# Storing the float32 copy of h from ScalarE's queue instead of SyncE's

## The chip, the cores and the metric

One Trainium2 chip, one core of it. The metric is the device time of one execution in microseconds; before and after are each given as a median of several executions. Beside the timed executions there is one profiled execution of the kernel before, and everything that is read from a trace comes from that one.

## What is computed

One decoder layer over 1024 tokens of 1024 channels, in float32. The part around the change is its beginning:

```python
ada = jax.nn.silu(c) @ w_ada + b_ada
shift, scale, gate = jnp.split(ada, 3, axis=-1)
h = _rmsnorm(x, norm_w) * (1.0 + scale[:, None, :]) + shift[:, None, :]
proj = jnp.einsum("bsd,de->bse", h, w_in)
z_ssm, xbc, dt_raw, q, k, v, z_att, f_logit, g_logit = jnp.split(proj, offsets, axis=-1)
y_ssm = _ssd_branch(z_ssm, xbc, dt_raw, conv_w, conv_b, dt_bias, a_log, d_skip, ssm_norm_w)
y_att = _fox_branch(q, k, v, z_att, f_logit, b_f)
g_ssm, g_att = jnp.split(jax.nn.sigmoid(g_logit + b_gate), N_BRANCHES, axis=-1)
merged = g_ssm * jnp.einsum("bse,ed->bsd", y_ssm, w_proj_ssm) + g_att * jnp.einsum("bse,ed->bsd", y_att, w_proj_att)
x = x + gate[:, None, :] * jnp.einsum("bsd,de->bse", merged, w_out)
return _rmsnorm(x, final_norm_w)
```

So h needs the row norms of x (over channels) and the two vectors scale and shift, which are products of silu(c) with a 1024 x 2048 matrix. All that follows is products of h with w_in, a state-space branch, an attention branch and the closing products.

## The kernel before, in words

Every product is done in split precision: a float32 matrix is cut into a high part (`hi`, a cast on ScalarE, L98) and a low part (`lo`, a subtraction on VectorE, L99), and TensorE forms hi·hi, hi·lo and lo·hi. Such a triple is L111, L112, L113 in `c_half`.

The opening stage builds h, transposed: eight blocks `k` of 128 channels, each in two halves `hf` of 512 tokens. Its parts are:

- Loads, all from SyncE's queue: eight pieces of x (`xt`, L209, 512 KB each), eight pieces of w_ada (`wa`, L213, 1 MB each, in five buffers), and the weights of the first three slabs (`wr`, L217).
- Row norms (L257 to L261): ScalarE squares and sums a piece of x (`sq`), VectorE and GpSimd form the factor `rs`, ScalarE scales the piece in place (L261). Eight pieces.
- `ada_cols(k)`: VectorE multiplies and adds eight pieces of one `wa` tile (L285 once, L287 seven times, into `acc`), two one-column products on TensorE sum it over partitions (`cp`, L289), VectorE forms the columns `av` and `sv` (L292, L294).
- `h_half(k, hf)`: four transposes on TensorE into the single buffer `tp` (L300), the activation that scales and shifts and writes `xa` in float32 (L303, ScalarE, four buffers), the store of `xa` to `h_scr` in DRAM (L304), the cast to the high part `hh` (L305, ScalarE) and the subtraction to the low part `hl` (L306, VectorE). That is 16 halves, so 16 stores of 256 KB.
- While h grows, TensorE multiplies each finished half with the first three slabs (L111 to L113 into the banks `mm` and `um`).

The float32 copy `h_scr` is read back once, at the start of the next stage, by `t_forms` (L441), which forms differences of blocks of h.

The program hands its instructions to a scheduler (`schedule_with_timeline_sim=True`), which writes one list per engine; each engine runs its list in order. DMAs are issued from such a list too, here all from SyncE's. The build also deals the DMAs out, one after the other, over eight completion counters, `DMAHW0` to `DMAHW7`. A DMA waits for its counter before it is issued: for the DMA that had the counter eight places before it.

Of the kernel before, what the change touches and what calls it, by code (L numbers as in the profile page):

```python
# [65 lines left out]
def build(ctx, tc, t):  # L66
    nc = tc.nc
    V, A, G, PE, SP = nc.vector, nc.scalar, nc.gpsimd, nc.tensor, nc.sync
# [7 lines left out]
    def f32(ap):  # L76
        return ap.bitcast(F32)
# [88 lines left out]
    h_scr = [dram.tile([P, S], F32, name=f"h_scr{k}") for k in range(NK)]  # L166
# [27 lines left out]
    def w_in(n, i, p):  # L194
        if (n, i, p) in ws_scr:
            return unit(ws_scr[n, i, p], 512)
        return unit(t["w_" + n][p + 4 * (i == 4), i % 2 == 0 and 1 or 0], 512)


    with tc.tile_pool(name="st", bufs=1, side="right") as st, \  # L200
# [95 lines left out]
        def h_half(k, hf):  # L296
            fs = slice(hf * 512, (hf + 1) * 512)
            tp = stp.tile([P, 512], F32, tag="tp", bufs=1, name="tp")
            for i in range(4):
                PE.transpose(out=tp[:, i * P:(i + 1) * P], in_=xts[4 * hf + i][:, k * P:(k + 1) * P],  # L300
                             identity=ident)
            xa = st.tile([P, 512], F32, tag="xa", bufs=4, name="xa")
            A.activation(out=xa, in_=tp, func=AF.Identity, scale=av[:, k:k + 1], bias=sv[:, k:k + 1])  # L303
            SP.dma_start(out=h_scr[k][:, fs], in_=xa)  # L304
            A.copy(out=hh[k][:, fs], in_=xa)  # L305
            V.tensor_tensor(out=hl[k][:, fs], in0=xa, in1=f32(hh[k][:, fs]), op=ALU.subtract)  # L306

        for k in range(2):
            ada_cols(k)
            h_half(k, 0)  # L310
        for k in range(2):
            h_half(k, 1)
        for k in range(2, 8):
            ada_cols(k)
            for hf in range(2):
                h_half(k, hf)
# [784 lines left out]
    with tc.tile_pool(name="finp", bufs=1, space=PSUM) as fpp_:  # L1101
# [66 lines left out]
        for i in ORDER:  # L1168
# [17 lines left out]
            else:  # L1186
                fs = [w_in("o", i, k) for k in range(4)]
# [65 lines left out]
```

## Time and profile before

| what | value |
|---|---|
| time, median of 3 executions | 1218.62 us (1217.94 to 1220.36) |
| the profiled execution | 1224.31 us, of it 1222.6 us span |
| busy: TensorE, VectorE, ScalarE, GpSimd | 1165.0, 955.9, 635.5, 88.4 us |
| mean granted TensorE clock | 0.988 |
| stores of `xa` (L304) | 16 of 256 KB, issued from 26.2 to 69.2 us |
| opening stage | from 0 to about 71 us of the span |

The span is what lies between the first and the last instruction of the profiled execution; 1.7 us of that execution's own time lie around it. That execution took 5.7 us more than the median of the timed ones. In rows of the timeline the first number is the start, the second the length, both in us; then engine, line and operation, output and input, and in brackets the idle time of the engine before it with what ended it. "SPq" and "ACTq" are the instruction lists of SyncE and ScalarE as far as they issue DMAs or wait. An `x7` at the end says that seven such instructions are drawn together.

### The profile page before, as it was taken

Reading aid. Unit: us, or ns where it says so; the run is one execution under the profiler, and the core shown is the slowest. Engines: PE = TensorE matmul, PEld = TensorE weight load, DVE = VectorE, ACT = ScalarE, POOL = GpSimd, SP = SyncE. Lnnn points to the kernel's source line nnn. Section 1 sums busy time; section 2 is a strip of 40 time slices with the busy share of each in tenths; the row PEclk is TensorE's granted clock in tenths of the full one; section 3 lists DMA queues with packets and bytes.
Section 4 is the critical chain, followed back from the end, with each engine's and each line's share of the span. In section 5 each row is a group of like instructions: output and inputs, shape, how many; then the busy total and the mean of one; then the engine's idle time right before and its main releaser. Section 6 shows DMA issues by size and latency. Waiting matters only on the chain.

```text
span 1222.6 us, 18382 instructions
## 1 busy us (share of the span) xinstructions
PE 1165.0 (95%) x6206; PEld 981.2 (80%) x6206; DVE 955.9 (78%) x1946; ACT 635.5 (52%) x1260; POOL 88.4 (7%) x152
## 2 busy tenths in 40 slices
PE   3999999999999999999999989999988999999997
PEld 2788888788877877998887778888877887788876
DVE  5856699788987784589999986664677977989967
ACT  7554443454443334776676633454456554454465
POOL 1000000000000000000000012222322220000001
PEclk9999999999999999999999989999998999999999
DMA  9665643655485676546545668422246526875334
GB/s 370 263 243 166 218 138 100 207 204 176 156 290 171 218 239 201 186 152 222 186 154 178 207 216 286 144 94 81 87 165 203 175 88 228 283 241 181 109 95 147
DMA packets 109018, 228.26 MB, mean 187 GB/s; under 512 B 12362, under 2 KB 20220, under 8 KB 107900
## 3 DMA queue, kind: packets, MB, share of 16 engines
q1 hardware_dynamic: 108924, 227.09, 55.2%
q8 instruction: 49, 0.80, 0.3%
q14 instruction: 45, 0.37, 0.1%
HBM read 159.14 MB, written 67.90 MB: 186 GB/s over the span
## 4 chain that ended last, share of the span: by engine, by line
PE 62%; DVE 16%; DMA 13%; ACT 4%; issue 4%; SPq 1%; POOL 0%; POOLq 0%; DVEq 0%; ACTq 0%
PE pp L497 4%; PE pv L1067 4%; PE pp L499 4%; PE pp L500 4%; PE lg L1036 3%; PE mm L497 3%; PE mm L499 3%; PE mm L500 3%; PE mm L112 3%; PE mm L113 3%; PE mm L111 3%; PE tp L1057 2%; DMA ab<-a_scr 2%; DMA wr<-w_c 2%; PE mm L919 2%
## 5 line engine op out<-in xcount | busy, mean ns | idle before, releaser
L98 ACT CAST wh<-wr 128x512 fp32r<-128x512 f32 (+1 forms) x214 | 131.0, 620 | 176.2 <-DMA wr<-w_c 32.4
L99 DVE TENSOR_TENSOR wl<-wr,wh 128x512 fp32r<-128x512 f32 (+1 forms) x214 | 146.9, 693 | 44.0 <-ACT wh L98 43.3
L112 PE MATMUL mm<-hl,wh 128*128 128x512 f32 x288 | 116.7, 405 | 0.4 <-DVE hl L306 0.4
L111 PE MATMUL mm<-hh,wh 128*128 128x512 f32 x288 | 116.2, 408 | 0.0
L113 PE MATMUL mm<-hh,wl 128*128 128x512 f32 x288 | 115.5, 402 | 0.0
L136 PE MATMUL mm<-wh,hh 128*128 128x256 f32 (+1 forms) x256 | 73.7, 289 | 1.9 <-DVE tmp L348 1.9
L137 PE MATMUL mm<-wl,hh 128*128 128x256 f32 (+1 forms) x256 | 74.4, 291 | 0.0
L138 PE MATMUL mm<-wh,hl 128*128 128x256 f32 (+1 forms) x256 | 73.7, 289 | 0.0
L1042 ACT ACTIVATE pr<-pr,sm 128x1024 f32<-128x1024 f32 (+3 forms) x64 | 49.9, 780 | 42.4 <-DVE sm L1041 35.1
L1060 ACT CAST pth<-tp 128x512 fp32r<-128x512 f32 (+1 forms) x80 | 42.4, 543 | 47.7 <-PE tp L1057 39.5
L1037 DVE CUSTOM_DVE_ANT_0 pr<-lg,fb 128x512 f32<-128x512 f32 (+1 forms) x96 | 51.4, 552 | 17.0 <-PE lg L1036 12.4
L112 PEld LDWEIGHTS mm<-hl,wh 128*128 128x128 f32 x288 | 55.2, 192 | 11.0 <-DVE hl L306 1.0
L113 PEld LDWEIGHTS mm<-hh,wl 128*128 128x128 f32 x288 | 55.0, 191 | 10.4
L111 PEld LDWEIGHTS mm<-hh,wh 128*128 128x128 f32 x288 | 54.7, 193 | 10.2 <-ACT hh L305 0.3
L690 ACT ACTIVATE ab<-ab,acs 128x128 f32<-128x128 f32 x128 | 41.2, 391 | 40.7 <-DMA ab<-a_scr 40.5
L1045 POOL TENSOR_SCALAR pr<-pr,sm 128x1024 f32<-128x1024 f32 (+3 forms) x64 | 51.8, 811 | 87.5 <-DVE sm L1044 70.2
L1061 DVE TENSOR_TENSOR ptl<-tp,pth 128x512 fp32r<-128x512 f32 (+1 forms) x80 | 50.0, 632 | 10.3 <-ACT pth L1060 10.2
L98 ACT CAST sh<-sr 128x512 fp32r<-128x512 f32 x57 | 34.0, 619 | 43.8 <-DVE sr L479 32.4
L796 POOL TENSOR_TENSOR fl<-fl,mhalf 128x8 f32<-128x8 f32 x1 | 1.6, 1647 | 698.2 <-DVE fl L794 698.2
L136 PEld LDWEIGHTS mm<-wh,hh 128*128 128x128 f32 x256 | 48.8, 191 | 2.4 <-DVE tmp L348 2.2
L1067 PE MATMUL pv<-pth,vh 128*128 128x256 f32 (+1 forms) x160 | 45.8, 287 | 4.5 <-DVE zg L1070 3.8
L138 PEld LDWEIGHTS mm<-wh,hl 128*128 128x128 f32 x256 | 49.1, 192 | 0.0
(407 smaller groups left out, 3509.8 us busy)
## 6 DMA issues: line engine op xcount, KB each, us to landing
wr<-w_c SPq DMA_DIRECT2D x116, 256.0 KB, 3.9
wa<-w_ada SPq DMA_DIRECT2D x8, 1024.0 KB, 11.4
g_scr<-gt SPq DMA_DIRECT2D x16, 512.0 KB, 4.2
ab<-a_scr SPq DMA_DIRECT2D x32, 256.0 KB, 3.9
gt<-g_scr SPq DMA_DIRECT2D x32, 256.0 KB, 3.7
wr<-w_ps SPq DMA_DIRECT2D x28, 256.0 KB, 2.6
wr<-w_pa SPq DMA_DIRECT2D x28, 256.0 KB, 2.8
wr<-so SPq DMA_DIRECT2D x28, 256.0 KB, 2.7
```

The lines of the kernel that those rows point to most:

```text
L98: A.copy(out=hi[:, :n], in_=raw[:, :n])
L99: eng.tensor_tensor(out=lo[:, :n], in0=raw[:, :n], in1=f32(hi[:, :n]), op=ALU.subtract)
L111: PE.matmul(ps, lhsT=hi[:, cs], rhs=xh[k][:, hs], start=(k == 0), stop=False)
L112: PE.matmul(ps, lhsT=hi[:, cs], rhs=xl[k][:, hs], start=False, stop=False)
L113: PE.matmul(ps, lhsT=lo[:, cs], rhs=xh[k][:, hs], start=False, stop=(k == 7))
L136: PE.matmul(o, lhsT=xh[k][:, ts], rhs=hi[:, cs], start=(k == 0), stop=False)
L137: PE.matmul(o, lhsT=xh[k][:, ts], rhs=lo[:, cs], start=False, stop=False)
L138: PE.matmul(o, lhsT=xl[k][:, ts], rhs=hi[:, cs], start=False, stop=(k == 7))
L497: PE.matmul(ps, lhsT=f[0][:, w], rhs=xh[:, hs], start=(first and k == 0), stop=False, skip_group_check=True)
L499: PE.matmul(ps, lhsT=f[0][:, w], rhs=xl[:, hs], start=False, stop=False, skip_group_check=True)
L500: PE.matmul(ps, lhsT=f[1][:, w], rhs=xh[:, hs], start=False, stop=(k == 3), skip_group_check=True)
L1067: PE.matmul(pv[:, o0:256], lhsT=x[kb // 4][:, kb % 4, vs], rhs=y[:, d:d + m], start=(kb == 0 and i == 0), stop=(kb == 2 * qq + 1 and i == 2))
```

## The change

The store at L304 is issued from ScalarE's list instead of SyncE's:

```diff
             xa = st.tile([P, 512], F32, tag="xa", bufs=4, name="xa")
             A.activation(out=xa, in_=tp, func=AF.Identity, scale=av[:, k:k + 1], bias=sv[:, k:k + 1])
-            SP.dma_start(out=h_scr[k][:, fs], in_=xa)
+            A.dma_start(out=h_scr[k][:, fs], in_=xa)
             A.copy(out=hh[k][:, fs], in_=xa)
             V.tensor_tensor(out=hl[k][:, fs], in0=xa, in1=f32(hh[k][:, fs]), op=ALU.subtract)
```

The scheduler then writes other lists, and three places matter.

First, ScalarE, right behind the first activation of the opening stage (`xa_421`, block 0, first half). Names are tiles with their buffer numbers; the bracket names the counters that the row waits for, `DMAHW7` being the one that the load `wa_292` used before. In the kernel before:

```order
L305 CAST hh0_240<-xa_421 128x512 [waits Activation_49]
L257 ACTIVATE sq_348,ss_323<-xt_282 128x1024 [waits DMAHW2_49]
L257 ACTIVATE sq_354,ss_323<-xt_284 128x1024 [waits DMAHW3_49]
L261 ACTIVATE xt_282<-xt_282,rs_350 128x1024 [waits Activation_49,Pool_49]
L257 ACTIVATE sq_360,ss_323<-xt_286 128x1024 [waits DMAHW4_49]
L261 ACTIVATE xt_284<-xt_284,rs_356 128x1024 [waits Activation_49,Pool_49]
L257 ACTIVATE sq_366,ss_323<-xt_288 128x1024 [waits DMAHW5_49]
L98 CAST e2_388<-wr_280 128x512 [waits DMAHW1_49]
L303 ACTIVATE xa_445<-tp_440,sv_373,av_372 128x512 [waits DVE_49,PE_49]
L261 ACTIVATE xt_286<-xt_286,rs_362 128x1024 [waits Activation_49,Pool_49]
L261 ACTIVATE xt_288<-xt_288,rs_368 128x1024 [waits Activation_49,Pool_49]
L305 CAST hh1_241<-xa_445 128x512 [waits Activation_49]
```

The same place in the changed kernel, again right behind the activation that writes `xa_421`:

```order
L304 DMA h_scr0_179<-xa_421 128x512 [waits DMAHW7_49,Activation_49]
L257 ACTIVATE sq_348,ss_323<-xt_282 128x1024 [waits DMAHW2_49]
L305 CAST hh0_240<-xa_421 128x512
L257 ACTIVATE sq_354,ss_323<-xt_284 128x1024 [waits DMAHW3_49]
L261 ACTIVATE xt_282<-xt_282,rs_350 128x1024 [waits Activation_49,Pool_49]
L257 ACTIVATE sq_360,ss_323<-xt_286 128x1024 [waits DMAHW4_49]
L303 ACTIVATE xa_445<-tp_440,sv_373,av_372 128x512 [waits DVE_49,PE_49]
L261 ACTIVATE xt_284<-xt_284,rs_356 128x1024 [waits Activation_49,Pool_49]
L257 ACTIVATE sq_366,ss_323<-xt_288 128x1024 [waits DMAHW5_49]
L98 CAST e2_388<-wr_280 128x512 [waits DMAHW1_49]
L261 ACTIVATE xt_286<-xt_286,rs_362 128x1024 [waits Activation_49,Pool_49]
L304 DMA h_scr1_180<-xa_445 128x512 [waits DMAHW1_49,Activation_49]
```

The first store now stands directly behind its activation, ahead of the norms of the last four pieces of x and of the first cast to `hh`; behind the last row shown come the cast of `hh1_241` and then the scaling of `xt_288`.

Second, SyncE, around the same stores; `wa_304` and `wa_306` are the loads of the seventh and eighth pieces of w_ada, `wr_844` and those after it the next stage's first weights. A minus marks rows of the kernel before that are gone from this list:

```order
 L217 DMA wr_298<-w_c 128x512
-L304 DMA h_scr0_179<-xa_421 128x512
 L213 DMA wa_304<-w_ada 128x2048
-L304 DMA h_scr1_180<-xa_445 128x512
-L304 DMA h_scr0_179<-xa_455 128x512
-L304 DMA h_scr1_180<-xa_465 128x512
 L213 DMA wa_306<-w_ada 128x2048
 L85 DMA wr_844<-w_v0 128x560
 L85 DMA wr_850<-w_v0 128x560
 L85 DMA wr_856<-w_v0 128x560
-L304 DMA h_scr2_181<-xa_489 128x512
 L85 DMA wr_862<-w_v0 128x560
```

The loads keep their order, and no store stands between them any more; the other stores are gone from the rows after these in the same way.

Third, VectorE between the second low part of block 2 and the first of block 3 (`hl_250` and `hl_251`). Before:

```order
L306 TENSOR_TENSOR hl_250<-xa,hh_242 128x512
L287 SCALAR_TENSOR_TENSOR acc<-wa,cols,acc 128x256 x7
L306 TENSOR_TENSOR hl_250<-xa,hh_242 128x512
L287 SCALAR_TENSOR_TENSOR acc<-wa,cols,acc 128x256 x2
L306 TENSOR_TENSOR hl_251<-xa,hh_243 128x512
```

In the changed kernel, from the second `hl_250` on:

```order
L306 TENSOR_TENSOR hl_250<-xa,hh_242 128x512
L287 SCALAR_TENSOR_TENSOR acc<-wa,cols,acc 128x256
L292 SCALAR_TENSOR_TENSOR av<-cp,cols 128x1
L294 TENSOR_TENSOR sv<-cp,cols 128x1
L285 TENSOR_SCALAR acc<-wa,cols 128x256
L287 SCALAR_TENSOR_TENSOR acc<-wa,cols,acc 128x256 x2
L99 TENSOR_TENSOR wl<-wr,wh 128x560
L287 SCALAR_TENSOR_TENSOR acc<-wa,cols,acc 128x256
L292 SCALAR_TENSOR_TENSOR av<-cp,cols 128x1
L294 TENSOR_TENSOR sv<-cp,cols 128x1
L285 TENSOR_SCALAR acc<-wa,cols 128x256
L287 SCALAR_TENSOR_TENSOR acc<-wa,cols,acc 128x256 x4
```

Sums for later blocks have moved ahead of `hl_251`, which follows the last row. Elsewhere the lists differ at two more places, one pair of loads in the attention of the third head (SyncE's rows L812 and L1022 are exchanged) and the order of some casts and products in the closing product; GpSimd's list is the same.

## Prediction

> **What bounds the kernel now.** I read the page first, then the busy time by stretches of the opening stage, then the timelines of ScalarE, SyncE, VectorE and TensorE there. The page:
>
> ```profile
> span 1222.6 us, 18382 instructions
> PE 1165.0 (95%) x6206; PEld 981.2 (80%) x6206; DVE 955.9 (78%) x1946; ACT 635.5 (52%) x1260; POOL 88.4 (7%) x152
> ...
> PE 62%; DVE 16%; DMA 13%; ACT 4%; issue 4%; SPq 1%; POOL 0%; POOLq 0%; DVEq 0%; ACTq 0%
> ```
>
> TensorE is busy for 95% of the span, so whatever delays its dense work moves the end by as much. The change touches only the opening stage, so I look there, cut where the argument needs it (columns: length, then busy us and count for PE, PEld, DVE, ACT, POOL, then clock and DMA):
>
> ```profile
> 18.25:26.20 7.95, 4.71 (x15) 4.01 (x16) 3.68 (x13) 7.92 (x13) 2.44 (x4) 1.00 1.03 421
> 29.07:71.00 41.93, 41.15 (x205) 33.56 (x206) 31.83 (x77) 24.16 (x38) 0.00 (x0) 1.00 0.61 231
> 80.00:90.00 10.00, 8.06 (x51) 7.83 (x50) 9.27 (x19) 4.20 (x9) 0.00 (x0) 0.83 0.95 371
> ```
>
> From 18.25 to 26.20 us ScalarE is the full engine (7.92 of 7.95 us) and TensorE has gaps (4.71). From 29.07 to 71 us TensorE is full: 41.15 of 41.93 us, so at most 0.78 us can be made good there. Early on ScalarE sets the pace, later TensorE.
>
> **The change part by part.** *The store's wait.* What the store waited for on SyncE:
>
> ```profile
> 12.19 2.86 SPq L213 DMA_DIRECT2D wa<-w_ada  x2
> ...
> 26.20 0.33 SPq L304 DMA_DIRECT2D h_scr<-xa  x1
> 26.86 0.33 SPq L213 DMA_DIRECT2D wa<-w_ada  x1
> ...
> 33.48 0.33 SPq L213 DMA_DIRECT2D wa<-w_ada  x1
> ```
>
> ```profile
> SPq L304 <- DMA wa<-w_ada: 2.1, 1, 2.1
> ```
>
> ```profile
> wa<-w_ada SPq DMA_DIRECT2D x1, 1024.0 KB, 11.4
> ```
>
> The first of these is SyncE's timeline, the second its waits between 24.1 and 26.3 us, the third the landing time of the second load of the pair at 12.19. That load (`wa_292`) is issued at 12.19 + 2.86 - 0.33 = 14.7 us and lands 11.4 us later, at 26.1. The store goes out at 26.20, and its wait is put down to a `wa` load. That agrees with the lists: the store waits for `DMAHW7`, which `wa_292` had. The data of the store has nothing to do with that load. On SyncE this cost nothing; in the changed kernel the same wait stands in ScalarE's list. Nothing that SyncE issues ahead of it is moved, so `wa_292` lands at 26.1 again.
>
> What stands behind it on ScalarE, from the timeline:
>
> ```profile
> 17.45 0.78 ACT L303 ACTIVATE xa<-tp,sv,av 128x512 f32<-128x512 f32 x1
> 18.25 0.62 ACT L305 CAST hh<-xa 128x512 fp32r<-128x512 f32 x1
> 18.78 1.05 ACT L257 ACTIVATE sq<-xt 128x1024 f32<-128x1024 f32 x1
> ...
> 19.83 1.04 ACT L257 ACTIVATE sq<-xt 128x1024 f32<-128x1024 f32 x1
> ...
> 25.16 0.60 ACT L98 CAST e<-wr 128x512 fp32r<-128x512 f32 x1
> 25.66 0.77 ACT L303 ACTIVATE xa<-tp,sv,av 128x512 f32<-128x512 f32 x1
> 26.34 2.17 ACT L261 ACTIVATE xt<-xt,rs 128x1024 f32<-128x1024 f32 x2
> 28.42 0.60 ACT L305 CAST hh<-xa 128x512 fp32r<-128x512 f32 x1
> ```
>
> Does such a wait hold the engine? A wait of ScalarE's list ahead of an activation:
>
> ```profile
> L303 ACTq EVENT_SEMAPHORE  x14: 17/17/1991, 15.4 to 66.7; - x14
> ```
>
> ```profile
> 37.29 0.78 ACT L303 ACTIVATE xa<-tp,sv,av 128x512 f32<-128x512 f32 x1 [1.97 <-DVE sv L294]
> ```
>
> The longest wait of the list, 1.991 us, is the same 1.97 us for which the engine stood idle. So ScalarE stands from 18.25 to 26.20, 7.95 us, in the very stretch in which it was full. The rows give the starts from one instruction to the next: activation 0.80, cast to hh 0.53, square 1.05, scaling 2.08 / 2 = 1.04, cast `e` 0.50. For the issue I take SyncE's 0.33; the trace has no store issued by ScalarE, and its bounds are 0 and 0.38 (the row of all 16, below). Up to the cast of `hh1`, the changed list has: two issues 0.66, four squares 4.20, one cast 0.53, three scalings 3.12, one activation 0.80, one cast `e` 0.50, in sum 9.81. That cast starts at 26.20 + 9.81 = 36.0 instead of 28.42: **7.6 us later** (the wait and two issues, less one scaling that has moved behind it). Who waits for it: VectorE (the norms' factors and `hl`), GpSimd (`rs`) and TensorE, none of which has other work to fill the time, since TensorE's dense stretch begins with these products at 29.07.
>
> *TensorE's order.* Its timeline while slow and while fast:
>
> ```profile
> 33.08 0.63 PE L112 MATMUL mm<-hl,e 128*128 128x512 f32 x1
> 33.51 0.52 PE L113 MATMUL mm<-hh,e 128*128 128x512 f32 x1
> 33.86 0.62 PE L111 MATMUL um<-hh,wh 128*128 128x512 f32 x2
> ...
> 35.46 0.40 PE L112 MATMUL um<-hl,wh 128*128 128x512 f32 x1
> 35.69 0.39 PE L113 MATMUL um<-hh,wl 128*128 128x512 f32 x1
> ...
> 41.02 0.50 PE L112 MATMUL mm<-hl,wh 128*128 128x512 f32 x1 [0.44 <-DVE hl L306]
> ...
> 47.41 0.48 PE L112 MATMUL mm<-hl,wh 128*128 128x512 f32 x1
> ```
>
> A product takes 0.43 us from start to start up to about 33.9 us and 0.23 after. Before, the first `um` product came 33.86 - 28.42 = 5.4 us after the start of that cast. In the changed list the last transpose of the next half stands behind all nine products of `hh1`: cast 0.62, nine products 3.9, transpose 0.4, activation 0.80, issue 0.33, cast 0.62, in sum 6.7. That is **1.2 us more**; bounds 0 (the products already fast: 9 x 0.20 = 1.8 less) and 3.6 (twelve products more at the slow spacing, 12 x 0.20 = 2.4).
>
> The Trainium skill (TensorE: Matmul & The Clock Gate, Part 1) has the array at half clock until it has been busy for about 3.4 us. The trace agrees in kind (0.43 against 0.23), though the granted clock reads 1.00 throughout. By that rule the new gaps while TensorE waits for ScalarE keep it slow for longer, which is the upper of the two bounds; I keep the middle.
>
> *VectorE's order.* Rows around the low parts of blocks 2 and 3:
>
> ```profile
> 40.29 0.68 DVE L306 TENSOR_TENSOR hl<-xa,hh 128x512 fp32r<-128x512 f32 x1
> 40.89 2.85 DVE L287 SCALAR_TENSOR_TENSOR acc<-wa,cols,acc 128x256 f32<-128x256 f32 x7
> 43.66 0.68 DVE L306 TENSOR_TENSOR hl<-xa,hh 128x512 fp32r<-128x512 f32 x1
> ...
> 45.06 0.68 DVE L306 TENSOR_TENSOR hl<-xa,hh 128x512 fp32r<-128x512 f32 x1
> ...
> 47.18 0.21 DVE L292 SCALAR_TENSOR_TENSOR av<-cp,cols 128x1 f32<-128x1 f32 x1
> ...
> 47.63 0.74 DVE L99 TENSOR_TENSOR wl<-wr,wh 128x560 fp32r<-128x560 f32 x1
> 48.28 2.04 DVE L287 SCALAR_TENSOR_TENSOR acc<-wa,cols,acc 128x256 f32<-128x256 f32 x4
> ```
>
> From the first `hl` of block 2 to that of block 3 passed 45.06 - 40.29 = 4.8 us. The changed list puts four more sums there (4 x 2.77 / 7 = 1.6 us), two groups of columns and a first product (0.45 each, 47.18 to 47.63) and one `wl` (0.65): 3.1 us more, 7.9 in all. TensorE needed 6.4 us for its own work between the two (its products with them start at 41.02 and 47.41) and gets 0.3 of columns more, so it waits about **1.2 us**; bounds 0 and 3.1.
>
> *The later stores.* Fourteen issues stand ahead of their casts, up to 0.38 us each:
>
> ```profile
> L304 SPq DMA_DIRECT2D h_scr<-xa x16: 319/320/383, 26.2 to 69.2; - x16
> ```
>
> ```profile
> ACT xa L303 <- PE tp L300: 12.7, 10, 2.9
> ```
>
> ScalarE waited 12.7 us for transposes in that stage, which covers fourteen issues (5.3 us at most): I cost them at nothing. Without that cover, each would push its cast and cost up to 5.3 us. One of them waits for the counter of `wa_306`, which by my count is issued at 40 us, with the store due at 48. The load at 33.48 landed in 9.1 us:
>
> ```profile
> wa<-w_ada SPq DMA_DIRECT2D x1, 1024.0 KB, 9.1
> ```
>
> So 40 + 9.1 - 48, about 1 us, is at stake there. *SyncE's list* loses its waits, and the last `wa` and the first weights of the next stage may leave earlier; nobody waits for them on TensorE before 71 us. The exchanges further on I cost at nothing, within some 2 us either way (the size of the single wait in the row of the first rival): which of their waits end last is not to be read from lists.
>
> The sum: 7.6 + 1.2 + 1.2 = 10.0 us. The profiled execution took 1222.6 us of span and 1.7 around it; with 10.0 more it would take 1234.3. It is 5.7 above the median of 1218.62, so the forecast goes on the median: **1228.6 us**.
>
> **The rivals.** *Faster: the loads freed from the stores.* The place is SyncE: `wa` at 26.86 and 33.48 stood behind stores and left late. If ScalarE were not held, for example were the load of `DMAHW7` to land by 18 us, the next stage would find its data ready and this wait would go:
>
> ```profile
> PE mm L136 <- DVE tmp L348: 1.9, 1, 1.9
> ```
>
> With the 0.78 us above that is at most 2.7 us: 1215.9. It decides only if the counter is free within 2.7 us of 18.25. Against it stands the landing at 26.1.
>
> *No change: the store costs its issue time only.* Nothing on TensorE's path then moves, and the time stays at 1218.6. For it speaks that SyncE issued such stores in 0.33 us; against it the 1.97 us row. The Trainium skill (DMA: Bandwidth & Descriptors, "Issuing engines are not separate DMA queues") says that issuing from several engines only saves the sequencer's time for starting transfers; by it nothing is gained but SyncE's time. No run here shows a second issuing engine.
>
> *Half: the hold is absorbed.* TensorE's gaps before 29 us take up more than I count, and the waits of the first rival go as well: 7.6 - 2.7 = 4.9, 1223.5.
>
> *More: waits multiply.* The upper bounds of both orders, 7.6 + 3.6 + 3.1 = 14.3: 1232.9.
>
> **How the numbers follow.** Forecast (6 to 13 us slower) 0.75; more than that 0.06; half 0.10; no change 0.05; faster 0.04. A measurement of this kernel tells about 0.2% (2.4 us) from no change. So slower 0.91, same 0.05, faster 0.04. The range goes from the half case, 1223.5, to the upper bounds, 1233.0, and leaves out about 0.15.
>
> **What would show it.** Right: ScalarE idle from about 18.2 to 26.2 us behind the first `xa`, ended by a `wa` load; the cast of `hh1` near 36 us; TensorE's full stretch starting about 8 us later and ending near 81 instead of 71; the rest unchanged in length. Wrong: ScalarE squaring the fifth piece of x at 19 us, which is one of the first two rivals; or the hold there and the end less than 3 us later, which would mean slack that I did not find.

## The result and the profile after

The changed kernel took 1230.53 us (median of 6 runs, 1225.4 to 1233.06), the kernel before 1220.28 beside it (6 runs, 1217.94 to 1221.01): the ratio on record is 1.0078 with a 95% interval of 1.0054 to 1.0102 (the two medians alone give 1.0084). The forecast was 1228.6, which is 10.0 above the first median of before. The profiled execution took 1229.29 us, of it 1227.5 span, at a mean granted clock of 0.993 (before: 1224.31, 1222.6, 0.988). So the timed runs are 10.25 us apart and the profiled ones 5.0; why, is a question of its own below. Two later executions of the kernel before took 1734.67 and 1908.23 us at a granted clock of 0.619 and 0.563; they are left out of all that follows.

First the page of the changed kernel:

```profile
span 1227.5 us, 18378 instructions
PE 1161.4 (95%) x6206; PEld 977.3 (80%) x6206; DVE 953.6 (78%) x1946; ACT 633.8 (52%) x1260; POOL 87.1 (7%) x152
```

TensorE's busy time is 3.6 us less and the span 4.9 more: what was added is waiting. Where, is in the busy time of the three stretches that were shown of before:

```profile
18.25:26.20 7.95, 2.13 (x8) 1.64 (x8) 2.11 (x5) 0.37 (x1) 0.00 (x0) 1.00 1.03 418
29.07:71.00 41.93, 37.56 (x168) 29.18 (x168) 32.52 (x86) 25.51 (x40) 1.86 (x3) 0.96 0.58 208
80.00:90.00 10.00, 10.00 (x69) 9.32 (x69) 4.78 (x8) 7.15 (x13) 0.00 (x0) 1.00 0.76 228
```

From 18.25 to 26.20 ScalarE is busy for 0.37 us instead of 7.92, while the DMA engines move what they moved before (418 GB/s against 421). TensorE's full stretch has lost 3.6 busy us and 37 of its 205 products. ScalarE's timeline shows what stands there (`ACTq` is the issue of a store; in brackets the idle time and what ended it):

```profile
17.85 0.78 ACT L303 ACTIVATE xa<-tp,sv,av 128x512 f32<-128x512 f32 x1
26.63 0.34 ACTq L304 DMA_DIRECT2D h_scr<-xa  x1
27.02 1.06 ACT L257 ACTIVATE sq<-xt 128x1024 f32<-128x1024 f32 x1 [8.39 <-DMA wa<-w_ada]
...
32.37 1.14 ACT L261 ACTIVATE xt<-xt,rs 128x1024 f32<-128x1024 f32 x1
32.75 0.33 ACTq L304 DMA_DIRECT2D h_scr<-xa  x1
...
36.01 0.60 ACT L305 CAST hh<-xa 128x512 fp32r<-128x512 f32 x1
...
71.07 0.78 ACT L303 ACTIVATE xa<-tp,sv,av 128x512 f32<-128x512 f32 x1 [0.73 <-DVE hl L306]
71.88 0.33 ACTq L304 DMA_DIRECT2D h_scr<-xa  x1
72.25 0.62 ACT L305 CAST hh<-xa 128x512 fp32r<-128x512 f32 x1 [0.40 <-ACT xa L303]
```

The square behind the first store starts after 8.39 us of idle time, which a load of w_ada ends; in the kernel before, the same square started at 18.78 without a wait. The second store at 32.75 is issued while ScalarE is still scaling a piece of x (32.37 to 33.51): its list runs ahead of the arithmetic, and the next square, at 33.41, shows no idle time before it. A store straight behind its activation, as at 71.88, leaves 0.40 us between activation and cast; without a store it was 0.02 (17.45 + 0.78 to 18.25 in before). ScalarE's waits from 16 to 85 us, in all, times, longest:

```profile
ACT xa L303 <- PE tp L300: 12.1, 7, 2.7
ACT sq L257 <- DMA wa<-w_ada: 8.4, 1, 8.4
ACT hh L305 <- ACT xa L303: 4.8, 12, 0.4
```

One wait on a load, and twelve of 0.4 us behind stores. TensorE's products at the places that the prediction named, and VectorE's first low parts of blocks 2 and 3:

```profile
28.73 1.22 PE L111 MATMUL mm<-hh,wh 128*128 128x512 f32 x2 [7.19 <-ACT hh L305]
...
42.87 0.74 PE L111 MATMUL um<-hh,wh 128*128 128x512 f32 x2 [0.35 <-ACT hh L305]
...
50.68 0.39 PE L112 MATMUL mm<-hl,wh 128*128 128x512 f32 x1
...
58.36 0.50 PE L112 MATMUL mm<-hl,wh 128*128 128x512 f32 x1 [0.80 <-DVE hl L306]
```

```profile
49.00 0.69 DVE L306 TENSOR_TENSOR hl<-xa,hh 128x512 fp32r<-128x512 f32 x1
...
57.62 0.68 DVE L306 TENSOR_TENSOR hl<-xa,hh 128x512 fp32r<-128x512 f32 x1
```

The end of the opening stage is marked by SyncE's first load of `pe`, which waits for the last stores. It was at 71.36 us before; in the changed kernel:

```profile
81.55 1.75 SPq L441 DMA_DIRECT2D pe<-h_scr  x4
```

That is 10.2 us later.

### The profile page after: what moved, and what is told of

It reads as the page before. It is cut to its first block, busy times and chain, and to the rows that moved or that the text cites. A ratio compares the mean times of both kernels' runs of the same rounds, so it can differ in the third digit from the quotient of the medians.

```text
span 1227.5 us, 18378 instructions
## 1 busy us (share of the span) xinstructions
PE 1161.4 (95%) x6206; PEld 977.3 (80%) x6206; DVE 953.6 (78%) x1946; ACT 633.8 (52%) x1260; POOL 87.1 (7%) x152
## 4 chain that ended last, share of the span: by engine, by line
PE 62%; DVE 14%; DMA 13%; ACT 5%; issue 4%; SPq 1%; ACTq 0%; POOL 0%; POOLq 0%; DVEq 0%
PE pv L1067 4%; PE pp L497 4%; PE pp L499 4%; PE pp L500 4%; PE lg L1036 3%; PE mm L497 3%; PE mm L499 3%; PE mm L500 3%; PE mm L112 3%; PE mm L111 3%; PE mm L113 3%; DMA ab<-a_scr 2%; PE tp L1057 2%; DMA wa<-w_ada 2%; PE mm L919 2%
## 5 line engine op out<-in xcount | busy, mean ns | idle before, releaser
L137 PEld LDWEIGHTS mm<-wl,hh 128*128 128x128 f32 x256 | 48.2, 188 | 0.2
```

The source lines that it names most:

```text
L137: PE.matmul(o, lhsT=xh[k][:, ts], rhs=lo[:, cs], start=False, stop=False)
```

## The experiments

The theory: ScalarE is held at the first store, by a completion counter that a w_ada load has, and the rest follows. The main rival: every store on ScalarE costs (issue time, and the lists re-ordered around it). A second question came from the trace: how much of the opening's loss stays to the end. In all runs two marks show the opening stage: the start of the second block's cast (`hh1`), and the first `pe` load. "Timed" is the median less that of the kernel before beside it.

| kernel | cast of `hh1` | first `pe` load | timed, us | ratio, 95% |
|---|---|---|---|---|
| before; once more | 28.42; 28.72 | 71.36; 70.87 | 0; +1.8 | 0.9995 to 1.0028 |
| changed; once more | 36.01; 35.79 | 81.55; 81.31 | +10.3; +7.9 | 1.0054 to 1.0102; 1.0042 to 1.0086 |
| only the first store on ScalarE; once more | 35.64; 35.73 | 79.83; 80.09 | +5.4; +4.5 | 1.0029 to 1.0063; 1.0021 to 1.0054 |
| all but the first | 29.88 | 73.07 | -0.1 | 0.9985 to 1.0020 |
| all but the first four | 28.44 | 71.24 | -1.6 | 0.9970 to 1.0005 |
| all, another counter for the first | 32.00 | 74.89 | +2.8 | 1.0017 to 1.0049 |
| all, behind the cast | 36.25 | 78.40 | +6.6 | 1.0033 to 1.0067 |
| all on GpSimd; once more | 28.64; 28.73 | 71.55; 72.18 | -2.6; -2.6 | 0.9965 to 1.0002; 0.9963 to 0.9993 |

**All but the first four on ScalarE.**

```diff
-            A.dma_start(out=h_scr[k][:, fs], in_=xa)
+            (A if k >= 2 else SP).dma_start(out=h_scr[k][:, fs], in_=xa)
```

> The four stores of blocks 0 and 1 are issued from SyncE's queue again, the other twelve from ScalarE's. Theory 1 (ScalarE is held by the completion counter of a w_ada load that the first store has to wait for): the hold of 7.95 us is gone, ScalarE squares the fifth piece of x near 19 us, hh1's cast starts near 28.4 and not 36.0, the opening stage ends near 71 us and not 81, and the time is that of the kernel before within 2 us. Theory 2 (each store costs ScalarE issue time and the two re-ordered lists cost the rest): twelve of sixteen stores keep their cost, so about 12/16 of 10, 7.5 us slower.

Measured 1219.23 us (11 runs) against 1220.87 (32 runs). The hold is gone and with it the loss, although twelve stores still stand in ScalarE's list. The rival's 7.5 us are excluded: the interval ends at 0.6.

**Only the first on ScalarE.**

```diff
-            A.dma_start(out=h_scr[k][:, fs], in_=xa)
+            (A if (k, hf) == (0, 0) else SP).dma_start(out=h_scr[k][:, fs], in_=xa)
```

> Only the very first store is issued from ScalarE's queue, the other fifteen from SyncE's. Theory 1 (the hold by the counter at this one store): the full loss, 8 to 10 us slower than before, hh1's cast near 36 us. Theory 2 (issue time of every store): one sixteenth of the loss, 0.6 us, not to be told from no change.

ScalarE's timeline and SyncE's first `pe` load in this run:

```profile
26.26 0.34 ACTq L304 DMA_DIRECT2D h_scr<-xa  x1
26.65 1.06 ACT L257 ACTIVATE sq<-xt 128x1024 f32<-128x1024 f32 x1 [8.38 <-DMA wa<-w_ada]
...
35.64 0.60 ACT L305 CAST hh<-xa 128x512 fp32r<-128x512 f32 x1
```

```profile
79.83 1.75 SPq L441 DMA_DIRECT2D pe<-h_scr  x4
```

One store out of sixteen brings the whole hold (8.38 us) and 8.5 of the 10.2 us by which the opening is late. In time it cost 5.4 us, less than the 8 to 10 expected, and far from the rival's 0.6.

**All but the first on ScalarE**, the complement.

```diff
-            A.dma_start(out=h_scr[k][:, fs], in_=xa)
+            (SP if (k, hf) == (0, 0) else A).dma_start(out=h_scr[k][:, fs], in_=xa)
```

> The first store goes from SyncE's queue, the other fifteen from ScalarE's: the complement of the run with the first store alone. Theory 1: no hold, hh1's cast near 28.8 us, the opening stage ends between 71.4 and 73.1 (at most the 1.7 us by which the changed kernel's opening was longer than that of the run with the first store alone), the time within 2 us of before. Theory 2 (each store on ScalarE costs): 15/16 of the loss, 9 us slower.

Measured 1221.17 against 1221.23 us (the interval goes from -1.8 to +2.4 us): no loss from fifteen stores. The opening is 1.7 us late, the cast of `hh1` comes at 29.88 instead of the expected 28.8, and ScalarE's timeline shows two small holds of the same kind:

```profile
29.50 0.34 ACTq L304 DMA_DIRECT2D h_scr<-xa  x1
29.88 0.62 ACT L305 CAST hh<-xa 128x512 fp32r<-128x512 f32 x1 [1.20 <-DMA wa<-w_ada]
...
39.64 0.62 ACT L305 CAST hh<-xa 128x512 fp32r<-128x512 f32 x1 [1.26 <-DMA wa<-w_ada]
```

Here the second store is the one that meets a load's counter too early, by 1.2 us. The cost is where the counter is late, not in the number of stores.

**Another counter for the first store.** Two small loads (20 and 8 KB) go from GpSimd, which has counters of its own. They are gone from the DMAs that are dealt over `DMAHW0` to `DMAHW7`, so every later one takes the counter two places before its old one.

```diff
-        SP.dma_start(out=hb, in_=t["heads"].broadcast_to([P, 40]))
+        G.dma_start(out=hb, in_=t["heads"].broadcast_to([P, 40]))
...
-        SP.dma_start(out=dsb, in_=t["d_skip"].broadcast_to([P, 16]))
+        G.dma_start(out=dsb, in_=t["d_skip"].broadcast_to([P, 16]))
```

> All sixteen stores stay on ScalarE's queue; the two small loads heads and d_skip are issued from GpSimd, so that the first store takes another completion counter, one that a load of x had (xt, which lands near 20 us), and no longer that of the w_ada load that lands at 26.1. Theory 1: the hold is cut from 8 us to about 2 us, and the second store's counter, that of the w_ada load, is free by the time it is reached; hh1's cast near 30 us, 1 to 4 us slower than before instead of 10. Theory 2 (issue time, second queue, any store on ScalarE): as slow as the changed kernel, about 10 us.

ScalarE's timeline:

```profile
20.13 0.78 ACT L303 ACTIVATE xa<-tp,sv,av 128x512 f32<-128x512 f32 x1
22.62 0.34 ACTq L304 DMA_DIRECT2D h_scr<-xa  x1
23.01 1.06 ACT L257 ACTIVATE sq<-xt 128x1024 f32<-128x1024 f32 x1 [2.10 <-DMA xt<-x]
...
32.00 0.61 ACT L305 CAST hh<-xa 128x512 fp32r<-128x512 f32 x1
```

With all sixteen stores on ScalarE, the hold is now 2.10 us, and what ends it is a load of x. The time is 2.8 us above before's: between 1 and 4, as expected, and not 10 (the interval goes from 2.1 to 6.0 us). My numbers for the way there were off (cast at 32.0 instead of 30): the first `xa` itself came 2.7 us later than in before (20.13 against 17.45). ScalarE's first square shows why, in this run and in before:

```profile
10.37 1.06 ACT L257 ACTIVATE sq<-xt 128x1024 f32<-128x1024 f32 x1 [2.38 <-DMA xt<-x]
```

```profile
7.68 1.06 ACT L257 ACTIVATE sq<-xt 128x1024 f32<-128x1024 f32 x1 [2.68 <-DMA xt<-x]
```

The first piece of x landed 2.7 us later, beside the two loads that now start early; that they are the reason is not shown. So the cast's 3.6 us are not the hold's alone, and this run bounds what its counter costs from above.

**The store behind the cast.**

```diff
-            A.dma_start(out=h_scr[k][:, fs], in_=xa)
             A.copy(out=hh[k][:, fs], in_=xa)
+            A.dma_start(out=h_scr[k][:, fs], in_=xa)
```

> All sixteen stores stay on ScalarE's queue, each behind the cast to hh instead of ahead of it. Theory 1 (the hold, wherever it stands in ScalarE's list, delays the four squares of the second half of x): the first store still waits for the load that lands at 26.1, hh0's cast is done before it but hh1's cast comes near 35.5 us instead of 28.4, TensorE does hh0's nine products inside a gap it would have had anyway, and the loss stays at 8 to 10 us. Theory 2 (the loss is the issue that stands between each activation and its cast, or the later stores): most of it goes, at most 2 us slower.

Measured 1227.83 us (8 runs) against 1221.23: 6.6 slower. ScalarE's timeline, and TensorE's longest wait from 26 to 110 us:

```profile
18.44 0.62 ACT L304 CAST hh<-xa 128x512 fp32r<-128x512 f32 x1
26.34 0.34 ACTq L305 DMA_DIRECT2D h_scr<-xa  x1
...
36.25 0.61 ACT L304 CAST hh<-xa 128x512 fp32r<-128x512 f32 x1
```

```profile
PE mm L111 <- ACT e L98: 10.9, 1, 10.9
```

The first cast is done before the hold and TensorE has six products more in the gap (nine were expected), but all that stands behind the store is late as before: only the name of the wait has changed. That falsifies the second theory (at most 2 us). The loss is 1.4 us under the lower end of my 8 to 10, though its interval (4.0 to 8.2 us) reaches it. TensorE's first `um` product, in before at 33.86, says where that is:

```profile
41.13 0.71 PE L111 MATMUL um<-hh,wh 128*128 128x512 f32 x2
```

The cast of `hh1` is 7.8 us late, this product 7.3, the whole opening 7.0: the two order terms of the prediction are not there with this list.

**All stores on GpSimd**, twice.

```diff
-            A.dma_start(out=h_scr[k][:, fs], in_=xa)
+            G.dma_start(out=h_scr[k][:, fs], in_=xa)
```

> All sixteen stores are issued from GpSimd's queue, whose first eight transfers have no earlier one to wait for; neither SyncE's loads nor ScalarE's activations stand behind a store. Theory 1: the time before, or up to 2.7 us faster if SyncE's loads, freed from the stores, are worth what the rival of the prediction gave them (the TensorE wait of 1.9 us near 83 us and 0.78 us of gaps). Theory 2 (stores beside the loads slow the loads): slower than before by more than 2.4 us.

> All sixteen stores from GpSimd's queue once more, to see whether it beats the kernel before: it gave 0.9965 to 1.0002. Theory 1 (the loads freed from the stores are worth something): 1 to 4 us faster again, its interval below 1. Rival (no difference, TensorE has no gap that these loads fill: its wait of 1.4 to 2.1 us for a tmp of VectorE near 83 us was there in every run): within 1 us of before.

1218.26 us against 1220.87, and 1218.65 against 1221.23: 2.6 us less both times, the second interval below 1 (0.9963 to 0.9993), the first just reaching it. So this version is about 0.2% faster than the kernel before, though only the second comparison shows it clearly, and it has no hold: in the first of these runs the first store left at 18.73 us, released by the activation that writes `xa` and not by a load. The mechanism that I named for it is not shown: the opening stage ends no earlier (71.55 and 72.18), and TensorE's wait for `tmp` is still there, 2.1 and 2.5 us. Where the 2.6 us come from stays open.

**The changed kernel, the first store alone and before, once more**, for the second question.

> The changed kernel once more, unaltered, beside the two runs that split it. Its opening stage ended 10.2 us later than before's in the profiles; the timed runs so far gave 1.0054 to 1.0102. Theory 1 (the whole of the opening's loss stays to the end): 9 to 11 us slower. Rival (a part of it is given back later, as the store-by-store runs hint: the run with only the first store on ScalarE lost 8.5 us in the opening and 5.4 in the timed median): 6 to 8 us slower. In either case its profile shows ScalarE idle for about 8.4 us behind the first xa and the first pe load near 81.5 us.

> Only the first store from ScalarE's queue, once more. Its opening stage was 8.5 us longer, its timed median 5.4 us. Theory (what the opening loses stays; the rest was chance of the runs): 7 to 9 us slower this time. Rival (about 3 us are given back further on, whenever the opening is late): 4 to 6.5 us slower again.

> The kernel before once more, for a second profile and as a zero of the comparison. Theory (the 2 us by which before's first profile lay behind at 104 us, beside a granted clock of 0.83 from 80 to 90, were a dip of the clock in that one execution; its opening stage is the same in every execution): first pe load again within 0.5 us of 71.4, ScalarE with no gap behind the first xa; without a dip there the wait of TensorE for tmp near 83 us stays at 1.4 to 2.5 us and the milestones at 104 us come about 2 us sooner. Rival (before really loses those 2 us, through SyncE's loads behind stores): 0.83 again and the same milestones within 0.5 us. The time: within 0.2% of itself.

The changed kernel measured 7.9 us slower this time, between the two forecasts, and its interval (5.1 to 10.5 us) decides nothing. Over all its runs the median is 1229.87 (12 runs), and before's is 1221.03 (the 90 runs beside the experiments): 8.8 us, on an opening that is 10.1 late. The first store alone gave 4.5 us again: the rival was right, about 4 us of its 8.6 are given back. So one store brings most of the opening's loss, but in time only 4.6 us (21 runs) of 8.8. The other fifteen alone cost nothing (-0.1), so about 4 us appear only where both stand in ScalarE's list. No run shows how.

The third expectation fell as well. The dip of the clock that I took for chance is in both profiles of before, with the same milestones. First before's stretch from 80 to 90 us in the second profile, then single microseconds of the first one:

```profile
80.00:90.00 10.00, 7.93 (x50) 7.71 (x50) 9.28 (x20) 3.92 (x9) 0.00 (x0) 0.83 0.94 368
```

```profile
80.00:84.00 4.00, 2.06 (x17) 1.83 (x16) 4.00 (x9) 2.68 (x6) 0.00 (x0) 1.00 1.03 415
84.00:85.00 1.00, 1.00 (x9) 1.00 (x9) 1.00 (x3) 0.00 (x0) 0.00 (x0) 0.98 1.03 418
85.00:86.00 1.00, 1.00 (x7) 1.00 (x6) 1.00 (x3) 0.62 (x1) 0.00 (x0) 0.50 1.05 404
86.00:87.00 1.00, 1.00 (x6) 1.00 (x6) 1.00 (x3) 0.00 (x0) 0.00 (x0) 0.50 1.03 397
...
88.00:89.00 1.00, 1.00 (x9) 1.00 (x8) 0.69 (x2) 0.33 (x2) 0.00 (x0) 0.81 0.89 336
```

TensorE waits from 80 to 84 us (2.06 us busy of 4, the `tmp` wait), and just behind that the granted clock is 0.50 for about 3.4 us (0.83 in the slice of ten: 10 x 0.17 / 0.50 = 3.4), which costs 1.7 us. The changed kernel has the same wait at 90 to 100 us (1.5 us) and no dip there, but one behind its waits at 41 to 43 us:

```profile
41.00:43.40 2.40, 1.51 (x9) 1.15 (x10) 2.09 (x8) 1.98 (x3) 0.00 (x0) 1.00 0.88 276
43.40:44.70 1.30, 1.30 (x11) 1.16 (x10) 1.29 (x5) 0.90 (x3) 0.00 (x0) 0.80 0.88 330
44.70:47.40 2.70, 2.70 (x8) 2.13 (x7) 2.69 (x9) 2.15 (x4) 0.00 (x0) 0.50 0.99 325
47.40:50.00 2.60, 2.60 (x15) 2.18 (x14) 2.60 (x6) 0.79 (x2) 0.00 (x0) 0.96 0.97 310
```

Whether a gap is followed by such a dip differs from kernel to kernel and from run to run: the stores on GpSimd have it at 80 to 90 us in one profile and not in the other. So part of what the kernels with the hold give back may be this. SyncE's first load of `w_ps` (L580, weights of a later stage) shows that part: it starts at 101.5 and 101.2 us in the two profiles of before and at 109.7 and 109.6 in those of the changed kernel. Of the 10.2 us at the end of the opening 8.2 are left by there, and the 2.0 that are gone are about what the dip behind 84 us costs before. At the first load of `w_o` (also L580; 372.3 and 380.4 us in the first two profiles) it is still 8.1. Further on the profiles decide nothing, since two of the same kernel differ as much: SyncE's last load of `ab` (L688, in the state-space branch) starts at 683.2 and 690.2 us in the two profiles of the first store alone.

An estimate from the mean granted clock goes further than it can be trusted. Before lost (1 - 0.988) x 1222.6 = 14.7 us to it, the changed kernel (1 - 0.993) x 1227.5 = 8.6, so 6.1 of the 10.2 us would have come back in the profiles. In the timed runs the mean granted clock is 0.9898 for before (90 runs), 0.9916 for the changed kernel (12) and 0.9928 for the first store alone (21). By the same sum (times 1221 us) that gives back 2.2 and 3.7 us, and 10.1 - 2.2 = 7.9 and 8.6 - 3.7 = 4.9 stand beside 8.8 and 4.6 measured. But for the store behind the cast (0.9885, 8 runs) the sum gives 7.0 + 1.6 = 8.6 and 6.6 were measured, for the other counter (0.9924, 12 runs) 3.5 - 3.2 = 0.3 against 2.8. And the two profiles of the first store alone, at 0.995 and 0.994, have spans of 1219.4 and 1226.8 us. The reading itself is not always the same for the same work. The stretch from 20 to 30 us, in before's first and second profile:

```profile
20.00:30.00 10.00, 6.29 (x18) 4.50 (x17) 5.66 (x18) 9.92 (x15) 2.44 (x4) 1.00 0.98 401
20.00:30.00 10.00, 6.05 (x19) 4.23 (x18) 5.66 (x18) 9.92 (x16) 2.45 (x4) 0.79 0.97 396
```

In both, TensorE's products are 0.43 us apart there, yet the clock reads 1.00 in one and 0.79 in the other (from 30 to 40 us 1.00 and 0.87). By the sum the second lost 3.4 us more; its opening ended 0.5 us earlier. Of the six profiles without a hold at the first store three read below 1 in these twenty microseconds, of the six with it none. So a part of the higher mean clock of the kernels with the hold may be no time at all, and where the rest of the give-back comes from stays open.

## Why the prediction was right, point by point

- **The hold.** Right. The first store waited for the load's counter; ScalarE stood for 8.39 us up to the next square (7.95 predicted up to the issue: the activation 17.85 + 0.78 = 18.63, the issue 26.63, thus 8.0). Giving the first store another counter cut it to 2.10 (two small loads are moved in that run as well), taking the one store away removed it: this cause is shown. The Trainium skill (Perfetto Trace Analysis, Per-engine timelines) lets an instruction of the sequencer alone wait in the sequencer, while an activation is pushed into a queue and the sequencer goes on. The trace agrees with both: the issue of a store waited in the list like the first, for 8.39 us, and the store at 32.75 was issued in the middle of a scaling.
- **The sum up to the cast of `hh1`.** Predicted 36.0, measured 36.01: 7.6 us late. That they agree so closely is luck: the issue came at 26.63 instead of 26.20 (this profile runs 0.4 us later than before's from the start, its first `xa` at 17.85 instead of 17.45), and from there to the cast it took 9.38 us instead of 9.81, mostly because the second issue, counted at 0.33, cost nothing.
- **TensorE's order.** Predicted 1.2 us and the first `um` product at 42.7; measured at 42.87, 33.86 before: 9.0, so 1.4 for this step. By the product of block 2's low part (50.68 against 41.02) it was 9.7: of the bounds 0 to 3.6 the step has taken 2.1. Part of it is the dip at 44.70 to 47.40, where products are 0.43 us apart again. The Trainium skill (TensorE: Matmul & The Clock Gate, Part 1), which pointed this way, has half clock after an idle window of about 3.4 us and until the array has been busy for about as long. The rows above agree in the half clock (0.50) and in the length of the dip (about 3.4 us), but not in what comes before it: TensorE had waited for 1.9 us ahead of the dip at 85 us, and for at most 0.53 at a time between 41 and 44.7 us.
- **VectorE's order.** Predicted 7.9 us between the two first `hl` and 1.2 of waiting; measured 57.62 - 49.00 = 8.6, a wait of 0.80, and the products 10.95 late (58.36 against 47.41), 1.3 more than at block 2. That was not the end: some 0.7 us came back by the end of the stage, which the sum did not have. In all 10.2 us, 0.4 of them the late start, against 10.0 predicted.
- **The later stores.** Predicted at nothing, and near the end of the opening that is what they cost. From 68.54 us on, `xa` follows `xa` every 2.53 us (71.07, 73.60, 76.12 in the changed kernel), as with the stores on SyncE:

```profile
71.80 0.78 ACT L303 ACTIVATE xa<-tp,sv,av 128x512 f32<-128x512 f32 x1 [1.10 <-PE tp L300]
...
74.34 0.78 ACT L303 ACTIVATE xa<-tp,sv,av 128x512 f32<-128x512 f32 x1 [1.10 <-PE tp L300]
```

  That is the run with the first store alone, 2.54 us apart. ScalarE's wait of 1.10 us has become one of 0.73; the store takes up the difference. So idle time covers the issues, as the prediction had it. The counter of `wa_306`, 1 us at stake, held nothing up. For the whole opening it is less clear: it ends 1.7 us later than with the first store alone (81.55 against 79.83). The dip between 43.4 and 50 us costs as much by the sum used above (0.26 + 1.35 + 0.10), and the run with the first store alone has none there (1.00 from 40 to 60 us); that it makes the difference is not shown.
- **SyncE's freed loads.** Predicted to be worth nothing before 71 us and little behind. In the changed kernel TensorE's wait for `tmp` is still 1.5 us (1.9 before). With the stores on GpSimd, where SyncE's loads are as free and nothing is held, it is 2.1 and 2.5: the first rival would not have removed it even without the hold. The Trainium skill's sentence on issuing engines, which saves the sequencer's time and nothing more (DMA: Bandwidth & Descriptors, "Issuing engines are not separate DMA queues"), fits the run with twelve stores on ScalarE (-1.6 us, not distinct from none); it says nothing of a counter.
- **The rest unchanged in length.** Too simple. The opening is 10.2 us longer as predicted, but what follows is shorter, by 5.3 us in the first profiles and by 1.3 in the medians of all runs. Some 2 us of it lie ahead of 110 us, where before has its dip; the rest is open. That the forecast of +10.0 met a first measurement of +10.25 is in part luck: all runs together give +8.8, which is the loss of the opening less a give-back that was not in the sum.

## What to carry to other kernels

Before a DMA is moved to a compute engine's queue, look at what it waits for besides its data: a wait that cost SyncE nothing holds every activation behind it, and a single early store can hold it for as long as all of them (8.38 and 8.39 us here). Give such an early transfer to an engine with no work behind it, or let the compute engine issue only transfers whose wait is over by then; the issue itself is small and, in this kernel, mostly hidden. Before a difference of a few us between two profiles is explained, take a second profile of each kernel: here two of the same kernel were 7.4 us apart.

## What the runs showed of the hardware

- ScalarE issues a store of 256 KB in 0.33 us, as SyncE does, and its list can issue it in the midst of an earlier activation; straight behind the activation that it depends on, it leaves 0.40 us between that and the next instruction, where 0.02 stand without it.
- A granted clock of 0.83 in a slice of ten microseconds was, at the two places looked into (80 to 90 us before, 40 to 50 us in the changed kernel), one stretch of about 3.4 us at 0.50, just behind waits of TensorE. The same kernel can have it or not, as with the stores on GpSimd.
- A granted clock that reads 1.00 is no proof of full speed: products 0.43 us apart stood beside 1.00 in one profile of the kernel before and beside 0.79 in the other.
- The runs of before spread from 1215.5 to 1226.6 us; how much of that the dips make is not shown.
